# All tensor-tensor arithmetic of GpSimd to VectorE, and the squares of x behind its split, in a decoder layer on one core

## The chip, the core and the metric

The kernel runs on one core of a Trainium2 chip. The core has five engines with a queue of instructions each: TensorE (PE in the profile; its weight loads are PEld), VectorE (DVE), ScalarE (ACT), GpSimd (POOL) and SyncE (SP), which here issues most DMAs. Each engine works through its queue in order; engines wait for each other by semaphores. The metric is the device time of one execution in microseconds (us), lower is better. Runs are compared by the median.

## The reference, cut to what matters

A decoder layer on 256 tokens of width 2048, in float32. Three stages follow each other, each with a normalization before and after it and a residual addition.

```python
h = rms_norm(x, mix_pre_norm)
proj = h @ w_in                                   # 2048 x 10536
mlstm_p, rwkv_p, gate_p = split_cols(proj, ...)
ha = sigmoid(o) * norm(mlstm_chunkwise(q, k, v, ig, logf))          # 4 heads, chunks of 64
hb = (groupnorm(rwkv7_scan(r, decay, kr, v, kk, kk * a)) + bonus) * g   # 16 heads of 64
y = (sigmoid(g_a) * (ha @ w_branch_a) + sigmoid(g_b) * (hb @ w_branch_b)) @ w_out
x = x + rms_norm(y, mix_post_norm)

h, m = rms_norm(x, xattn_pre_norm), rms_norm(mem, mem_norm)
x = x + rms_norm(softmax(q(h) @ k(m).T) @ v(m) @ wo, xattn_post_norm)   # 4 heads of 128, 256 memory tokens

h = rms_norm(x, ffn_pre_norm)
u = causal_conv3(h @ w_up)                        # 2048 x 16384
x = x + rms_norm((gelu(gate(u)) * up(u)) @ w_down, ffn_post_norm)      # 8192 x 2048
```

`rms_norm` needs the sum of squares of each token over 2048 features. In the kernel a token's scale is applied behind the product, so that the products with w_in can begin before the sum is known.

## The kernel before, in words

**Precision.** Each large product is made of three products in the fast float32 format: a weight tile `raw` from DMA is rounded to `wh` by ScalarE (line 344), VectorE makes the remainder `wl = raw - wh` (line 353), and TensorE adds up wh*xh, wh*xl and wl*xh, where xh and xl are the same split of the activation (`hh`, `hl` for x in the first stage; `qh`, `ql` behind the first residual, `fh`, `fl` behind the second).

**Weight tiles and blocks.** `run` walks a list of blocks. A block is a piece of a weight matrix; its weights come as tiles of 128 x 1024 (128 x 768 in the first block), which I number through the program. Tiles 0 to 7 are the small columns of w_in (block "sm", 18 products a tile); 8 to 103 the projections r, k, v, q and k of the mLSTM, its v and its o (two blocks of 8 tiles each); 104 to 199 the gates and the two branch products, of which branch b begins with tile 168; 200 to 231 w_out; 232 to 239 the key of the cross-attention, 240 to 247 its query, 248 to 255 its value, 256 to 263 its output; 264 to 519 the FFN's up projection (32 blocks of 8 tiles); 520 to 647 its down projection. Most tiles cost 24 products with 256 columns. `run` stages wh and wl three tiles ahead of the products; there are 3 buffers for raw and 4 each for wh and wl. A block's PSUM banks come from four called acc; a block needs two, so before a block is begun, `run` calls `side.need` for the evacuation of the block two before.

**The side work.** Everything else (evacuations, gates, the chunked mLSTM, the RWKV scan, softmax, statistics, residuals) is written as Python generators. `Spread` decides, while the program is being written, where their pieces stand between the products. At each half of a tile `half` adds 600 to a budget for VectorE and 820 for ScalarE. A piece of the first waiting bulk generator, or else of one of the first two of `back`, is written while both budgets are above 0; pieces of `chains` are written every so many halves as long as the budgets are above -700. What a piece costs is counted by `Meter`, which wraps ScalarE and VectorE (`act`, `dve`) and adds a fixed part and a part per element to `spent`. GpSimd (`pool`) is not wrapped. `need` writes all that is left of a generator at once, at the place where it is called:

```python
    def need(self, s):
        while s and not s["done"]:
            if s in self.bulk:
                self._piece(self.bulk[0])
            ...
```

`need_hb` calls it for both halves of `rwkv` and for `hb_split` in front of the block of tile 168; `need_o` for the softmax and its product with the values in front of tile 256; `run` for the evacuation of the first up block in front of tile 280.

**Where GpSimd computes.** In `x_piece` (line 455) it squares the eight pieces of x and adds up the squares in st0. In `k_group` (line 704), run four times, it makes four products: KR, k2 and two halves of BK. In `gates` it multiplies a mask into pw, in `mlstm` it adds two parts of pw. In `Residual` (line 1181) it adds z to the stream xr for six of eight parts, and in `Stat.add` (line 257), called from there with `pool`, it adds up the squares of the new stream (stx, stf). At the end of the kernel it makes one of the eight last additions (line 1590). Apart from these it makes the power -0.5 of `rstd_of` (line 225), small copies and memsets, and issues the loads of `gup` in `hb_split` (line 1085).

`pre_sm` (line 470) orders the first block: for each piece of x a split into hh and hl on ScalarE and VectorE, then the squares on GpSimd, with the loads of x and of the weights on SP between. `sm_evac` (line 504) finishes the statistics (`finish`: one sum on VectorE, a product with ones on TensorE, `rstd_of`, a product that spreads the row) and reads the first block's banks.

`rwkv` (line 853) is written once for each half of the heads. Each pair of chunks ends in a group normalization: sum, subtraction, squares (ScalarE), sum, power (GpSimd), product, transposes (TensorE), scaling (ScalarE) and an addition to `bv`. When both halves are through, `hb_split` starts: split of gl, loads of gup, their split into gwh and gwl, four products zg, and for each a product with bv and the split into hb.

Of the kernel before, what the change touches and what calls it, by code (L numbers as in the profile page):

```python
# [11 lines left out]
AF = mybir.ActivationFunctionType  # L12
ALU = mybir.AluOpType
# [132 lines left out]
def _layer(ctx, tc, nc, d, dbg):  # L146
    act, dve = Meter(nc.scalar, 200.0, 0.83), Meter(nc.vector, 70.0, 1.04)
    pool, pe, sp = nc.gpsimd, nc.tensor, nc.sync
# [42 lines left out]
    xq = [x0[c // 4][:, c % 4 * 2:c % 4 * 2 + 2] for c in range(8)]  # L191
# [5 lines left out]
    def pcol(n, i=0, w=1):  # L197
        return par[:, PC[n] + i:PC[n] + i + w]

    def ccol(n, w, o=0):  # L200
        return con[:, CC[n] + o:CC[n] + o + w]

    ident = ccol("id", 128)
    E2 = [slice(0, 64), slice(64, 128)]
# [34 lines left out]
    def bc(ap, n):  # L239
        return ap.unsqueeze(1).broadcast_to((ap.shape[0], n, ap.shape[1]))  # L240

    class Stat:
# [11 lines left out]
        def square(self):  # L254
            return C("sq", f"{self.sq}{self.n % 2}", [P, 2, S])

        def add(self, src, eng=None):
            if self.n == 0:
                self.start()
                act.activation(self.acc, src, AF.Square)  # L260
            else:
                q = self.square()
                act.activation(q, src, AF.Square)
                (eng or dve).tensor_add(self.acc, self.acc, q)
            self.n += 1

        def fold(self):
# [185 lines left out]
    st0 = Stat("st0")  # L453

    def x_piece(c):
        for j in range(2):
            split_gain(hh[:, c * 2 + j], hl[:, c * 2 + j], xq[c][:, j], pcol("mixg", c * 2 + j))
        if c == 0:
            st0.start()
            pool.tensor_mul(st0.acc, xq[c], xq[c])  # L460
        else:
            q = st0.square()
            pool.tensor_mul(q, xq[c], xq[c])
            pool.tensor_add(st0.acc, st0.acc, q)
        st0.n += 1

    def x_load(c):
        sp.dma_start(xq[c], d["x"][:, c * 2:c * 2 + 2])
# [1 line left out]
    def pre_sm(ci, feed):  # L470
        if ci == 0:
            keep_warm(12)
            for c in range(3):
                x_piece(c)
                feed.lo(c)
                feed.dma(c + 3)
                x_load(c + 4)
            x_load(7)
        if ci + 3 < 8:
            x_piece(ci + 3)  # L480
        if ci == 4:
            sp.dma_start(con, d["con"])

# [6 lines left out]
    M, tasks = {}, {}  # L490
# [13 lines left out]
    def sm_evac(ps):  # L504
        dve.tensor_scalar(om, pcol("mu", 0, 27), -1.0, 1.0, op0=ALU.mult, op1=ALU.add)
        dve.tensor_scalar(oka, pcol("ka", 0, 8), -1.0, 1.0, op0=ALU.mult, op1=ALU.add)
        yield from st0.finish(3)
        pr = PR()
        dve.tensor_mul(pr, ps[0], bc(st0.rb, 2))
        wa, gl = C("wa", "m0"), T2("gl")  # L510
        gl0, gl1 = gl[:, 0], gl[:, 1]
        shiftmix(wa, pr[:, 0], 24)
        shiftmix(gl0, pr[:, 1], 25)
        yield
        pr = PR()
        dve.tensor_mul(pr[:, 0], ps[1][:, 0], st0.rb)
        shiftmix(gl1, pr[:, 0], 26, slice(0, 32))
        R = [T2("rows") for _ in range(4)]
        M["rows"] = R
        tasks["gates"] = side.add(gates(), chain=1)  # L520
        act.copy(R[0][0:4, 0], pr[32:36, 0])
        act.copy(R[0][0:4, 1], pr[64:68, 0])
        act.activation(wa[0:64], wa[0:64], AF.Tanh)
        tasks["smr"] = side.add(sm_rest(wa, gl0, gl1), back=True)
        yield
# [41 lines left out]
    def gates():  # L567
# [19 lines left out]
        src, alt = R4[4], R4[5]  # L587
# [72 lines left out]
        for o in (0, 256):  # L660
            for e in range(2):
                v = pw[E2[e], :, o + e * 64:o + e * 64 + 64]
                pool.tensor_mul(v, v, bc(ccol("im", 64)[E2[e]], 4))
            pool.memset(pw[E2[1], :, o:o + 64], 0.0)
        yield

# [37 lines left out]
    def k_group(p0):  # L704
        yield from side.patience(tasks["smr"], 60)
        KR, BK, at, lw, rr = M["KR"], M["BK"], M["at"], M["lw"], M["rr"]
        ss = slice(p0, p0 + 2)
        yield from side.patience(tasks["gates"], 60)
        if p0 == 0:
            tables("natural_log_exp_and_others")  # L710
        if p0 % 4:
            kt = U("kt", [P, 4, 2, S])
            k2, kk, nr, ep = (kt[:, i] for i in range(4))
        else:
            kt = [C("kt", f"au{i}", [P, 2, 2, S]) for i in range(2)]
            k2, kk, nr, ep = (kt[i // 2][:, i % 2] for i in range(4))
        kr = BK.rearrange("p a c s t -> p a (c s t)")[:, ss, 0:S]
        f8 = lambda v: v.rearrange("p a (c t) -> p (a c) t", c=4)
        KR8, BK8 = (v[:, ss].rearrange("p a c s t -> p (a c) s t") for v in (KR, BK))
        cum = lw[:, ss]  # L720
        for j in range(2):
            dve.tensor_tensor_scan(cum[:, j], seg, cum[:, j], 0.0, op0=ALU.mult, op1=ALU.add)
        for j in range(2):
            act.activation(kk[:, j], kr[:, j], AF.Identity, scale=pcol("kk", p0 + j))
        act.activation(nr, kk, AF.Square)
        q = yield from head_sums("ssk", nr)
        dve.tensor_scalar(nr, q, 1e-24, None, op0=ALU.max)
        act.activation(ep, cum, AF.Exp, scale=DECAY)
        yield
        act.activation(nr, nr, AF.Ln)  # L730
        act.activation(nr, nr, AF.Exp, scale=-0.5)
        yield
        for j in range(2):
            act.activation(k2[:, j], at[:, p0 + j], AF.Identity, scale=pcol("ka", p0 + j), bias=oka[:, p0 + j:p0 + j + 1])
        dve.tensor_mul(kk, kk, nr)
        pool.tensor_mul(KR8[:, :, 1], f8(rr[:, ss]), f8(ep))
        dve.scalar_tensor_tensor(KR8[:, :, 0, 1:64], f8(kk)[:, :, 1:64], -1.0, f8(ep)[:, :, 0:63],
                                 op0=ALU.mult, op1=ALU.mult)
        pool.tensor_scalar(KR8[:, :, 0, 0], f8(kk)[:, :, 0], -1.0, None, op0=ALU.mult)
        pool.tensor_copy(pce[:, ss], ep.rearrange("p a (c t) -> p a c t", c=4)[:, :, :, 63])  # L740
        pool.tensor_mul(k2, kr, k2)
        yield
        act.activation(nr, cum, AF.Exp, scale=-DECAY)
        dve.tensor_mul(kk, kk, at[:, ss])
        yield
        for e in range(2):
            dve.tensor_mul(BK8[E2[e], :, e], f8(kk)[E2[e]], f8(nr)[E2[e]])
            pool.tensor_mul(BK8[E2[e], :, 1 - e], f8(k2)[E2[e]], f8(nr)[E2[e]])
        yield
        for j in range(2):  # L750
            dve.scalar_tensor_tensor(rr[:, p0 + j], rr[:, p0 + j], pcol("rk", p0 + j), k2[:, j], op0=ALU.mult, op1=ALU.mult)
        yield
# [280 lines left out]
    def mlstm():  # L1033
        pw, vm, so = M["pw"], M["vm"], M["so"]
        M["pws"] = T2("pws")
        pool.tensor_add(M["pws"].rearrange("p a b -> p (a b)").rearrange("p (h q) -> p h q", h=4),
                        pw[:, :, 128:256], pw[:, :, 256:384])
        for t in range(2):
            js = [0] if t == 0 else [0, 1]
            qd = aux("den", [P, 4])  # L1040
# [137 lines left out]
    def part(v, k2):  # L1178
        return v[k2 // 4][:, (k2 % 4) * 2:(k2 % 4) * 2 + 2]

    class Residual:
# [8 lines left out]
        def run(self):  # L1190
# [24 lines left out]
            def scale(i):  # L1215
                dve.tensor_mul(part(z, i), part(z, i), bc(rb, 2))

            def add(i, eng):
                eng.tensor_add(part(xr, i), part(xr, i), part(z, i))  # L1219

            if self.early:
                yield
# [7 lines left out]
            yield  # L1230
            for i in range(1, 8):
                if i == 1:
                    add(1, dve)
                if i < 7:
                    scale(i + 1)
                    add(i + 1, pool)
                parts(i)
                if i == 1 and not self.early:
                    side.more()
                if self.early:  # L1240
                    self.st2.add(part(xr, i - 1), pool)
                elif i == 6:
                    self.stats = side.add(self.squares(0), chain=1)
                yield
# [3 lines left out]

        def squares(self, i0):
            for i in range(i0, 8):  # L1250
                self.st2.add(part(M["xr"], i), pool)
                yield
            for _ in range(2):
                yield
            yield from self.st2.finish(2)
# [307 lines left out]
    def fd_evac(n):  # L1563

        def gen(ps):
# [19 lines left out]
            def result(t, c):  # L1585
                f = slice(c % 2 * 512, c % 2 * 512 + 512)
                x, z_ = M["xt"][c // 2][:, t, f], M["z3", c // 2][:, t, f]
                if t and c == 1:
                    act.activation(z_, z_, AF.Copy, scale=rco[:, t:t + 1])
                    pool.tensor_add(x, x, z_)  # L1590
                else:
                    dve.scalar_tensor_tensor(x, z_, rco[:, t:t + 1], x, op0=ALU.mult, op1=ALU.add)
                (act if t and c != 1 else sp).dma_start(d["out"][t, :, c * 512:c * 512 + 512], x)

            if n == 0:
# [121 lines left out]
```

## Time and profile before

| | |
|---|---|
| median of 3 runs | 1953.44 us (1952.64 to 1955.28) |
| the profiled execution | 1954.48 us |
| its span from first to last instruction | 1952.6 us |
| mean granted clock of TensorE | 0.995 |
| busy: TensorE, VectorE, ScalarE, GpSimd | 1914.5, 1345.7, 1001.2, 136.7 us |
| instructions on VectorE, ScalarE, GpSimd | 1789, 1434, 127 |
| read from HBM | 347.73 MB, 179 GB/s over the span |

The profile is one execution. A row of the timeline has the start, the duration, the engine, the source line and the operation, then "out<-in" by the program's names, the shape and the count; in brackets stands how long the engine was idle before and what ended that. Nearly all rows of ScalarE and VectorE have line 66, that of Meter's wrapper, so that names and shapes tell them apart. A row of the groups has busy time and mean duration in ns of one. "A <- B: 16.1, 13, 2.2" among the waits means that A waited 16.1 us for B in 13 waits, the longest 2.2 us. Chain rows have start, length and count.

### The profile page before, as it was taken

To read this page: it belongs to the slowest core of one execution; us is meant where nothing else is said; L and a number is where in the kernel's file an instruction comes from. 1 tells how busy PE (TensorE), PEld (TensorE's weight loads), DVE (VectorE), ACT (ScalarE), POOL (GpSimd) and SP (SyncE) were. 2 spreads that over 40 slices of the span, in tenths; PEclk is the share of its full clock that TensorE was granted. 3 is DMA by queue.
4 is the path that set the end of the run, shared out by engine and by line. 5 is a ranking of instruction groups with operands and counts; after the bars stand their busy time and mean duration, and the time that the engine had idled before them with its cause. 6 is when DMAs were issued, how large, how long until landed. Compare 5 with 4: busy or idle time off the path is not lost.

```text
span 1952.6 us, 36537 instructions
## 1 busy us (share of the span) xinstructions
PE 1914.5 (98%) x15084; PEld 1805.1 (92%) x15084; DVE 1345.7 (69%) x1789; ACT 1001.2 (51%) x1434; POOL 136.7 (7%) x127
## 2 busy tenths in 40 slices
PE   8999999999999999899999999999999999999998
PEld 7999986999999999888999999999999998888886
DVE  6879888575566665867767666776667675556555
ACT  4776434454454564555555445544454454445443
POOL 4213100000010000304000000000000000000000
PEclk8999999999999999999999999999999999999999
DMA  6555645344455675435555655555655655655554
GB/s 205 170 163 168 182 156 162 109 152 141 132 190 180 214 256 182 159 132 172 173 184 189 197 196 192 189 194 195 194 195 185 199 190 200 207 188 191 187 191 151
DMA packets 97606, 352.20 MB, mean 180 GB/s; under 512 B 10880, under 2 KB 11136, under 8 KB 97056
## 3 DMA queue, kind: packets, MB, share of 16 engines
q1 hardware_dynamic: 96496, 348.07, 54.5%
q8 instruction: 118, 1.93, 0.4%
q10 hardware_dynamic: 720, 1.15, 0.2%
q0 software_dynamic: 224, 0.66, 0.1%
q14 instruction: 48, 0.39, 0.1%
HBM read 347.73 MB, written 2.10 MB: 179 GB/s over the span
## 4 chain that ended last, share of the span: by engine, by line
PE 88%; DVE 6%; issue 2%; DMA 2%; ACT 2%; POOL 1%; SPq 0%; DVEq 0%; ACTq 0%; POOLq 0%
PE fm L181 62%; PE tm L181 21%; DVE wl L353 2%; DVE tmp L66 1%; DMA raw<-in_w_in_dram 1%; ACT wh L344 1%; DVE fl L66 1%; PE Y L181 1%; DVE hl L66 1%; DMA raw<-in_w_fu_dram 0%; PE gram L181 0%; PE lv L181 0%; DVE z L66 0%; DMA raw<-in_w_sm_dram 0%; POOL xr L1219 0%
## 5 line engine op out<-in xcount | busy, mean ns | idle before, releaser
L353 DVE TENSOR_TENSOR wl<-raw,wh 128x1024 fp32r<-128x1024 f32 (+1 forms) x648 | 810.4, 1252 | 445.5 <-ACT wh L344 441.9
L344 ACT CAST wh<-raw 128x1024 fp32r<-128x1024 f32 (+1 forms) x648 | 675.1, 1044 | 573.9 <-PE fm L181 378.6
L181 PE MATMUL fm<-fl,wh 128*128 128x256 f32 x2048 | 568.0, 277 | 1.4 <-DVE fl L66 1.3
L181 PE MATMUL fm<-fh,wh 128*128 128x256 f32 x2048 | 568.5, 278 | 0.8 <-ACT fh L66 0.8
L181 PE MATMUL fm<-fh,wl 128*128 128x256 f32 x2048 | 567.5, 277 | 1.0 <-DVE wl L353 1.0
L181 PEld LDWEIGHTS fm<-fl,wh 128*128 128x128 f32 x2048 | 385.2, 188 | 2.2 <-DVE fl L66 2.2
L181 PEld LDWEIGHTS fm<-fh,wl 128*128 128x128 f32 x2048 | 385.3, 188 | 1.2 <-DVE wl L353 1.2
L181 PEld LDWEIGHTS fm<-fh,wh 128*128 128x128 f32 x2048 | 385.4, 188 | 1.0 <-ACT fh L66 1.0
L181 PE MATMUL tm<-wh,as 128*128 128x512 f32 x1024 | 318.6, 392 | 0.0
L181 PE MATMUL fm<-hh,wl 128*128 128x256 f32 x1072 | 302.3, 282 | 10.9 <-DVE wl L353 10.9
L181 PE MATMUL fm<-hh,wh 128*128 128x256 f32 x1072 | 306.7, 286 | 1.2 <-ACT wh L344 1.2
L181 PE MATMUL fm<-hl,wh 128*128 128x256 f32 x1072 | 301.4, 281 | 0.0
L181 PEld LDWEIGHTS tm<-wh,as 128*128 128x128 f32 x1024 | 192.2, 188 | 43.6
L181 PEld LDWEIGHTS fm<-hh,wl 128*128 128x128 f32 x1072 | 204.0, 190 | 12.9 <-DVE wl L353 12.9
L181 PEld LDWEIGHTS fm<-hh,wh 128*128 128x128 f32 x1072 | 204.1, 190 | 4.6 <-ACT wh L344 1.7
L181 PEld LDWEIGHTS fm<-hl,wh 128*128 128x128 f32 x1072 | 204.1, 190 | 0.0
L181 PE MATMUL tm<-wl,as 128*128 128x512 f32 x512 | 201.0, 393 | 0.0
L181 PEld LDWEIGHTS tm<-wl,as 128*128 128x128 f32 x512 | 96.1, 188 | 21.7
L66 ACT CAST as<-ac 128x256 fp32r<-128x256 f32 x128 | 45.6, 404 | 118.1 <-PE tm L181 118.0
L66 DVE TENSOR_TENSOR as<-ac,as 128x256 fp32r<-128x256 f32 x128 | 48.6, 422 | 66.6 <-ACT as L66 66.5
L225 POOL TENSOR_TENSOR rco<-var,mhalf 128x1 f32<-128x1 f32 x2 | 1.1, 550 | 1019.9 <-DVE var L66 1019.9
L181 PE MATMUL fm<-mgh,wh 128*128 128x256 f32 x256 | 71.4, 279 | 0.0
(363 smaller groups left out, 2341.7 us busy)
## 6 DMA issues: line engine op xcount, KB each, us to landing
raw<-in_w_fu_dram SPq DMA_DIRECT2D x256, 512.0 KB, 4.3
raw<-in_w_in_dram SPq DMA_DIRECT2D x160, 512.0 KB, 3.6
raw<-in_w_fd_dram SPq DMA_DIRECT2D x128, 512.0 KB, 4.3
raw<-in_w_br_dram SPq DMA_DIRECT2D x32, 512.0 KB, 3.8
raw<-in_w_mo_dram SPq DMA_DIRECT2D x32, 512.0 KB, 3.9
raw<-in_w_xk_dram SPq DMA_DIRECT2D x8, 512.0 KB, 4.3
raw<-in_w_xq_dram SPq DMA_DIRECT2D x8, 512.0 KB, 3.7
raw<-in_w_xv_dram SPq DMA_DIRECT2D x8, 512.0 KB, 3.6
```

Source lines behind the costliest of these rows:

```text
L66: return f(out, *a, **k)
L181: pe.matmul(out, lhsT, rhs, start=start, stop=stop, skip_group_check=True)
L225: pool.tensor_tensor(out, v, mhalf[:, 0:out.shape[1]], op=ALU.pow)
L344: nc.scalar.copy(wh, r)
L353: nc.vector.tensor_sub(wl, r, self.st[self.nl][0])
```

## The change

Three things are done. Each GpSimd operation with two tensors as inputs (but for the power in `rstd_of`) is issued on VectorE with the same operands. The squares of x go out of `x_piece`: `st0.add` makes them on ScalarE and adds them up on VectorE, for the pieces 0 to 5 in `pre_sm` at the tiles 5 to 7, when all pieces have been split, and for 6 and 7 at the beginning of `sm_evac`, a piece of side work each. And the last addition of line 1590 with the scaling before it becomes the one VectorE operation that the other seven results have.

```diff
         def add(self, src):
             ...
                 q = self.square()
                 act.activation(q, src, AF.Square)
-                (eng or dve).tensor_add(self.acc, self.acc, q)
+                dve.tensor_add(self.acc, self.acc, q)
     def x_piece(c):
         for j in range(2):
             split_gain(hh[:, c * 2 + j], hl[:, c * 2 + j], xq[c][:, j], pcol("mixg", c * 2 + j))
-        if c == 0:
-            st0.start()
-            pool.tensor_mul(st0.acc, xq[c], xq[c])
-        else:
-            q = st0.square()
-            pool.tensor_mul(q, xq[c], xq[c])
-            pool.tensor_add(st0.acc, st0.acc, q)
-        st0.n += 1
...
         if ci + 3 < 8:
             x_piece(ci + 3)
+        else:
+            for c in range((ci - 5) * 2, (ci - 5) * 2 + 2):
+                st0.add(xq[c])
...
     def sm_evac(ps):
...
+        for c in (6, 7):
+            st0.add(xq[c])
+            yield
         yield from st0.finish(3)
...
-                pool.tensor_mul(v, v, bc(ccol("im", 64)[E2[e]], 4))
+                dve.tensor_mul(v, v, bc(ccol("im", 64)[E2[e]], 4))
...
-        pool.tensor_mul(KR8[:, :, 1], f8(rr[:, ss]), f8(ep))
+        dve.tensor_mul(KR8[:, :, 1], f8(rr[:, ss]), f8(ep))
...
-        pool.tensor_mul(k2, kr, k2)
+        dve.tensor_mul(k2, kr, k2)
...
-            pool.tensor_mul(BK8[E2[e], :, 1 - e], f8(k2)[E2[e]], f8(nr)[E2[e]])
+            dve.tensor_mul(BK8[E2[e], :, 1 - e], f8(k2)[E2[e]], f8(nr)[E2[e]])
...
-        pool.tensor_add(M["pws"]..., pw[:, :, 128:256], pw[:, :, 256:384])
+        dve.tensor_add(M["pws"]..., pw[:, :, 128:256], pw[:, :, 256:384])
...
-            def add(i, eng):
-                eng.tensor_add(part(xr, i), part(xr, i), part(z, i))
+            def add(i):
+                dve.tensor_add(part(xr, i), part(xr, i), part(z, i))
...
-                    add(i + 1, pool)
+                    add(i + 1)
...
-                    self.st2.add(part(xr, i - 1), pool)
+                    self.st2.add(part(xr, i - 1))
...
-                self.st2.add(part(M["xr"], i), pool)
+                self.st2.add(part(M["xr"], i))
...
             def result(t, c):
-                if t and c == 1:
-                    act.activation(z_, z_, AF.Copy, scale=rco[:, t:t + 1])
-                    pool.tensor_add(x, x, z_)
-                else:
-                    dve.scalar_tensor_tensor(x, z_, rco[:, t:t + 1], x, op0=ALU.mult, op1=ALU.add)
+                dve.scalar_tensor_tensor(x, z_, rco[:, t:t + 1], x, op0=ALU.mult, op1=ALU.add)
```

More of the change, by code (lines that the diff above doesn't have):

```diff
@@ L255, in square, with add @@
             return C("sq", f"{self.sq}{self.n % 2}", [P, 2, S])
-        def add(self, src, eng=None):
+        def add(self, src):
             if self.n == 0:
@@ L1035, in mlstm @@
         M["pws"] = T2("pws")
-        pool.tensor_add(M["pws"].rearrange("p a b -> p (a b)").rearrange("p (h q) -> p h q", h=4),
-                        pw[:, :, 128:256], pw[:, :, 256:384])
+        dve.tensor_add(M["pws"].rearrange("p a b -> p (a b)").rearrange("p (h q) -> p h q", h=4),
+                       pw[:, :, 128:256], pw[:, :, 256:384])
         for t in range(2):
@@ L1232, in run @@
                 if i == 1:
-                    add(1, dve)
+                    add(1)
                 if i < 7:
                     scale(i + 1)
-                    add(i + 1, pool)
+                    add(i + 1)
                 parts(i)
```

## The prediction

> **What bounds the kernel now.** I read the page's shares first, then the waits of TensorE, then its busy time in windows, then the timelines of the places where it is idle.
>
> ```profile
> PE 1914.5 (98%) x15084; PEld 1805.1 (92%) x15084; DVE 1345.7 (69%) x1789; ACT 1001.2 (51%) x1434; POOL 136.7 (7%) x127
> PE 88%; DVE 6%; issue 2%; DMA 2%; ACT 2%; POOL 1%; SPq 0%; DVEq 0%; ACTq 0%; POOLq 0%
> PE fm L181 <- DVE wl L353: 16.1, 13, 2.2
> PE st L181 <- DVE stf L66: 2.4, 1, 2.4
> 585.16 130.32 PE fm L181 x1128
> ```
>
> TensorE is busy for 98% of the span and carries 88% of the chain that ended last. The change touches none of its products, so the time can move only where TensorE stands still: 1952.6 - 1914.5 = 38 us in all. It mostly waits for VectorE's weight remainder (wl). The last row prices its work: 130.32 / 1128 = 0.1155 us a product, 2.8 us for a weight tile of 24. Where it stands:
>
> ```profile
> 0.00:36.60 36.60, 27.67 (x169) 0.86 0.59 191
> 165.00:170.00 5.00, 2.99 (x26) 1.00 0.34 108
> 170.00:175.00 5.00, 5.00 (x31) 0.66 0.70 215
> 300.00:330.00 30.00, 26.12 (x120) 1.00 0.48 154
> 800.00:816.20 16.20, 11.03 (x88) 1.00 0.40 136
> 875.00:900.00 25.00, 21.76 (x175) 1.00 0.32 106
> ```
>
> The columns are the stretch, its length, TensorE's busy time, its matmuls, the granted clock, the DMA share and GB/s. The stops sit at the start, near 167, around 300 to 330 (the inverses), and in the two residual stages. All but the third lie where GpSimd works beside VectorE.
>
> **The change part by part.** First what VectorE pays for GpSimd's company, in the first block:
>
> ```profile
> 17.86 2.68 DVE L66 SCALAR_TENSOR_TENSOR hl<-x,par,hh 128x256 fp32r<-128x256 f32 x2
> 20.34 1.32 POOL L464 TENSOR_TENSOR st<-st,sq 128x512 f32<-128x512 f32 x1
> 20.47 2.01 DVE L353 TENSOR_TENSOR wl<-raw,wh 128x768 fp32r<-128x768 f32 x1
> 30.20 0.95 DVE L353 TENSOR_TENSOR wl<-raw,wh 128x768 fp32r<-128x768 f32 x1
> 31.07 0.87 DVE L66 SCALAR_TENSOR_TENSOR hl<-x,par,hh 128x256 fp32r<-128x256 f32 x2
> 31.86 0.95 DVE L353 TENSOR_TENSOR wl<-raw,wh 128x768 fp32r<-128x768 f32 x1
> ```
>
> With GpSimd active a piece of x costs VectorE 2.68 + 2.01 = 4.7 us; with GpSimd quiet (after 28 us) it costs 31.86 - 30.20 = 1.66 us. TensorE needs 18 x 0.1155 = 2.1 us for a piece, so today VectorE sets the pace and the 144 products of the block end only at 36.6 us (169 matmuls there, 24 of them warm-up). After the change VectorE needs 1.66 a piece and TensorE sets the pace: first product at 7.2, about 0.9 us for the first remainder, then 144 x 0.1155 = 16.6, so about 24.7, a gain of 11.9. Two things eat into it: the loads must come faster, and eight squares on ScalarE with seven additions on VectorE (0.6 us each) now stand between the weight tiles 8 to 12. They fit into ScalarE's idle time there, and cost at most some 1 us. I take -10.5, with -12 and -4 as ends (loads at 191 GB/s bring 5.3 MB only by 30 us).
>
> The operations in k_group: four products of 512 columns and two mask lines. Without GpSimd beside it VectorE needs 0.6 us for each. The stop at 165 to 170 (2.0 us) and the slower clock behind it, (1 - 0.66) x 5 = 1.7 us, should go: -3.7. At 300 to 330 GpSimd is idle, and VectorE has the same 31 growing steps after the change; they only come some 16 weight tiles later: 0, between -3.9 and +4.
>
> The early residual, between the key and the query block:
>
> ```profile
> 776.15 0.68 DVE L66 TENSOR_TENSOR z<-z,stb 128x512 f32<-128x512 f32 x1
> 776.75 0.88 DVE L66 SCALAR_TENSOR_TENSOR ql<-xr,par,qh 128x256 fp32r<-128x256 f32 x2
> 777.81 1.22 DVE L353 TENSOR_TENSOR wl<-raw,wh 128x1024 fp32r<-128x1024 f32 x1 [0.19 <-ACT wh L344]
> 778.96 0.68 DVE L66 TENSOR_TENSOR xr<-xr,z 128x512 f32<-128x512 f32 x1
> 789.62 1.91 DVE L66 SCALAR_TENSOR_TENSOR ql<-xr,par,qh 128x256 fp32r<-128x256 f32 x2
> 789.78 1.47 POOL L1219 TENSOR_TENSOR xr<-xr,z 128x512 f32<-128x512 f32 x1 [1.76 <-DVE z L66]
> 791.46 2.32 DVE L353 TENSOR_TENSOR wl<-raw,wh 128x1024 fp32r<-128x1024 f32 x1
> ```
>
> A part now takes 0.6 + 1.9 + 2.3, about 4.7 us with starts overlapping. Afterwards it is z, xr, ql, the statistics' addition and wl: 0.6 + 0.6 + 0.8 + 0.6 + 1.15 = 3.75 us. That is above TensorE's 2.8, but eight parts run up 8 x 0.95 = 7.6 us, less than the three weight tiles (8.3 us) by which run() stages ahead. The 16.2 - 11.0 = 5.2 us go. The late residual has no statistics: 0.6 + 0.6 + 0.8 + 1.15 = 3.15 a part against 3.56 now; of its 3.2 us about 2.0 go.
>
> **What the accounting does.** Meter adds to spent for ScalarE and VectorE alone. What moves from GpSimd becomes visible to Spread, which then gives side work out more slowly. The order of the changed program's instructions shows the result: whole chains that stood between products now stand in one lump, directly in front of the block that needs them. The first lump is the hand-over to branch b (weight tile 168). All of the end of rwkv for both halves and the whole of hb_split stand there; before, only the last two zg groups did. Its steps:
>
> ```profile
> 541.99 0.68 DVE L66 TENSOR_REDUCE gv<-bg 128x8 f32<-128x512 f32 x1
> 543.02 2.51 POOL L225 TENSOR_TENSOR gr<-var,mhalf 128x8 f32<-128x8 f32 x1 [3.32 <-DVE var L66]
> 546.24 0.69 DVE L66 TENSOR_TENSOR ysb<-ysb,gr 128x512 f32<-128x512 f32 x1
> 548.76 1.50 ACT L66 ACTIVATE bg<-yT,par 128x128 f32<-128x128 f32 x4 [0.87 <-PE yT L975]
> gup<-in_g_up_dram POOLq DMA_DIRECT2D x2, 256.0 KB, 5.5
> 566.26 1.78 ACT L66 CAST gwh<-gup 128x512 fp32r<-128x512 f32 x3
> 578.02 0.62 ACT L66 CAST hb<-vT 128x512 fp32r<-128x512 f32 x1 [1.89 <-DVE vT L66]
> 578.67 0.69 DVE L66 TENSOR_TENSOR hb<-vT,hb 128x512 fp32r<-128x512 f32 x1 [0.69 <-ACT hb L66]
> 583.24 1.91 PE zg L181 x16
> ```
>
> From TensorE's last product before it: about 0.9 for VectorE's previous remainder, then gv 0.7, power 0.3 + 2.5, product 0.7, transposes 0.6, four scalings 1.5, addition 0.7, and some 0.3 of hand-offs: 8.2. The other half follows in VectorE's order, 7.3 more, so 15.5. The loads of gup are issued behind the second power, at 11.7, and land 5.5 later, at 17.2; casts and remainder bring 19.4, two zg groups 21.3. The products with zg, cast and remainder of two groups end at about 23.9 for ScalarE, which then casts the second gup (1.8, 25.7); its remainder at 26.0, the last two zg groups at 28.0. Of this 1.2 of transposes and 3.8 of zg are TensorE's own work and stood elsewhere before: 23 us of stop. The clock: after a stop of 2 us this trace shows 5 us at 0.66. I add 3 us for zg and the first products at a lower clock: +26, between 20 and 31.
>
> The second lump is the softmax in front of weight tile 256. Statistics of the early residual end later, so four heads stand there in a row:
>
> ```profile
> 825.08 1.02 PE L181 MATMUL xsc<-kT,qT 128*128 128x256 f32 x4
> 827.12 1.28 ACT L66 ACT_TABLE_LOAD   x1 [1.01 <-DVE mx L66]
> 830.19 0.68 DVE L66 TENSOR_REDUCE mx<-xsc 128x2 f32<-128x512 f32 x1
> 832.96 0.69 DVE L66 TENSOR_REDUCE mx<-xsc 128x2 f32<-128x512 f32 x1
> L181 PE MATMUL xsc<-kT,qT 128*128 128x256 f32 x16 | 4.1, 379 | 0.0
> L181 PE MATMUL xo<-pT,xv 128*128 128x256 f32 x16 | 4.0, 392 | 0.1
> L1414 PE MATMUL xpT<-con,spr 128*128 128x128 f32 x16 | 2.4, 275 | 0.4 <-DVE spr L66 0.4
> ```
>
> The first scores come after 1.6 us, their maximum at 2.5; from the table load to the second head's maximum it is 830.19 - 827.12 = 3.1, so 5.6; then 832.96 - 830.19 = 2.8 a head, the fourth maximum at 11.2; its exponentials, scaling and transposes end at 14.7; xo ends at 18.7. TensorE's own share is 4.1 + 2.4 + 4.0 = 10.5, so 8.2 of stop, and 3 for the clock: +11.2, between 7 and 16.
>
> Two smaller ones. At weight tile 72 the banks of the first query block are read later than before, two remainders and two such products behind the last k_group's: +1.6. In front of tile 280 the statistics of the FFN input are forced, with four additions: about 4 us of stop where now the wait for stf (2.4) and that for its power stand: 0, between -1 and +2. At the very end one addition leaves GpSimd: -0.4.
>
> The sum: 26 + 11.2 + 1.6 - 10.5 - 3.7 - 5.2 - 2.0 - 0.4 = +17.0. The profiled execution took 1954.5 us (span 1952.6, the rest around it), so 1971.5; the runs' median, 1953.4, lies 1.0 lower: 1970.
>
> The clock is the term that I know least. The Trainium skill, page TensorE: Matmul & The Clock Gate, section "What's actually happening", says that the array falls to half its clock after about one idle window of 3.4 us and needs a busy one to come back. By that rule each lump would pay its own products at half rate and up to 3.4 us of products behind it, an estimate of 1.7 us for each such window. The trace agrees as far as it goes, with 0.66 over 5 us behind the stop at 167; no row of it has a stop of 10 us.
>
> **The rivals.**
> Faster: the first lump costs little. The place is tile 168, the condition that its two halves and the gup loads run beside each other and beside products, so that TensorE stops for less than 26 - 17 = 9 us. At no cost the time is 1944. For it speaks that VectorE and ScalarE have spare time (69% and 51% busy); against it that VectorE's order puts the second half behind the first, and that every engine there waits for the next.
> Colder: at half clock TensorE's 15.5 us in the two lumps take twice as long, and most of that lies on the path, since it alternates with the others: some +10, 1980. For it speaks the 0.66, against it that several stops of 1.5 us between 800 and 816 left the clock at 1.00.
> Loads: the first block is then bound by DMA and gains 4, not 10.5: 1976. The 191 GB/s there is a mean over a time in which the loads waited for buffers, which speaks against it.
> Half price: both lumps are pushed back only partly, and cost half, 18.6 less: 1951, no change.
>
> **How the numbers follow.** Forecast 0.58, colder 0.16, loads 0.08, half price 0.08, first lump free 0.10. The range 1955 to 1986 takes in the ends of the two lumps and of the start, and leaves out the free lump, part of half price and the top of colder, about 0.2. A difference below 0.2% (3.9 us) can't be told from none here. Slower takes the first three and a little of half price, 0.84; same 0.05, faster 0.11. The forecast's own range is 1961 to 1980.
>
> **What would show it.** Right: GpSimd's rows are powers and small copies; wl of 768 columns takes 0.95 from the start; the 144th product of the first block ends near 25 to 27 us; no stop of TensorE near 800; one stop of 20 to 30 us, in pieces, in front of the first product that reads hb, one of about 8 in front of the first that reads oT, with a clock well below 1 in both. Wrong: the first product with hb follows the last one with hh within 10 us, or VectorE's wl ends later than today somewhere in the long up and down projections, where no instruction changes place.

## The result, and the profile after

The changed kernel takes 1979.15 us (median, 1977.83 to 1980.73), the kernel before on the same chip 1953.04 us (1949.84 to 1955.28): a ratio of 1.0131, with a 95% interval of 1.0119 to 1.0143. It is 26 us slower; 17 were forecast. The profiled execution has a span of 1978.9 us. Its first rows, engine by engine, and the chain that ended last:

```profile
PE 1926.5 (97%) x15084; PEld 1814.6 (92%) x15084; DVE 1328.4 (67%) x1844; ACT 1006.2 (51%) x1441; POOL 42.8 (2%) x64
PE 80%; DVE 4%; ACT 2%; issue 1%; POOL 0%; DMA 0%; DVEq 0%; POOLq 0%; ACTq 0%
```

TensorE's idle time went from 38 to 52.4 us, and its busy time rose by 12.0 us for the same 15084 instructions, so products ran slower too. VectorE is busy for 17.3 us less, though it runs 55 instructions more: without GpSimd beside it, they are shorter on average. What TensorE waited for:

```profile
PE yT L974 <- DVE ysb L66: 9.9, 2, 5.7
PE xpT L1413 <- DVE spr L66: 6.5, 4, 3.2
PE zg L181 <- ACT gwh L66: 5.5, 2, 3.2
PE fm L181 <- DVE wl L353: 3.4, 7, 0.8
PE st L181 <- DVE stf L66: 3.1, 1, 3.1
PE gram L181 <- DVE bg L66: 2.8, 2, 2.4
PE tm L181 <- DVE kT L66: 2.5, 1, 2.5
PE tm L181 <- DVE qk L66: 2.4, 1, 2.4
PE den L181 <- DVE rd L66: 1.3, 1, 1.3
```

The wait for wl, 16.1 us before, is down to 3.4. In its place stand waits inside the side work: the transposes of rwkv's tail (yT), the softmax (xpT), the products of hb_split (zg).

To apportion the 26 us, I numbered the weight tiles in both traces and took for each stretch of tiles TensorE's loss: the gaps between its products, and by how much each product exceeds the median of its kind before. What moves from one stretch to another without loss drops out.

| tiles | before | after | change | forecast | uncharged (below) | charged (below) |
|---|---|---|---|---|---|---|
| 0 to 23, start | 17.1 | 7.0 | -10.1 | -10.5 | 6.4 | 15.3 |
| 48 to 55, k_group | 3.7 | -0.3 | -4.0 | -3.7 | -0.3 | -0.3 |
| 56 to 91, banks at 72 | 1.3 | 5.1 | +3.8 | +1.6 | 1.3 | 6.4 |
| 92 to 165, inverses, mlstm, rwkv | 21.2 | 27.0 | +5.8 | 0 | 21.4 | 23.6 |
| 166 to 179, first lump | -0.2 | 22.7 | +22.9 | +26 | -0.2 | 24.2 |
| 240 to 247, early residual | 6.1 | 2.3 | -3.8 | -5.2 | 1.2 | 6.2 |
| 248 to 257, second lump | 1.5 | 12.0 | +10.5 | +11.2 | 1.5 | 10.6 |
| 258 to 271, late residual | 5.6 | 5.0 | -0.5 | -2.0 | 4.5 | 6.0 |
| 272 to 287, FFN statistics | 4.9 | 6.9 | +2.0 | 0 | 0.3 | 10.8 |
| the rest | 4.0 | 4.0 | 0 | -0.4 | 4.0 | 4.0 |
| sum | 65.2 | 91.7 | +26.5 | +17.0 | 39.9 | 106.7 |

One row needs care. What is left after the change in tiles 240 to 247 (2.3) is no stop of the residual: it is the wait of 2.5 us for kT, in front of the first product of tile 248, whose PSUM bank the late evacuation of the key block (kT) still has to read.

The windows that answer to those of before:

```profile
0.00:26.10 26.10, 23.33 (x168) 22.29 (x169) 16.03 (x27) 18.04 (x32) 1.44 (x12) 1.00 0.78 260
150.00:200.00 50.00, 50.00 (x435) 50.00 (x435) 41.15 (x56) 33.33 (x49) 2.32 (x4) 1.00 0.59 183
300.00:330.00 30.00, 29.37 (x147) 24.31 (x146) 29.55 (x30) 12.93 (x14) 0.00 (x0) 1.00 0.50 150
375.00:380.00 5.00, 4.44 (x25) 4.25 (x26) 2.97 (x7) 0.67 (x1) 0.00 (x0) 0.50 0.57 195
580.00:585.00 5.00, 1.09 (x4) 0.71 (x4) 1.57 (x4) 2.02 (x5) 0.44 (x1) 0.50 0.00 0
595.00:600.00 5.00, 2.54 (x9) 1.69 (x8) 3.32 (x6) 2.89 (x5) 0.00 (x0) 0.50 0.00 0
600.00:605.00 5.00, 5.00 (x30) 5.00 (x31) 2.31 (x4) 1.60 (x3) 0.00 (x0) 0.65 0.01 3
800.00:820.00 20.00, 20.00 (x174) 20.00 (x174) 19.51 (x29) 14.43 (x23) 0.00 (x0) 1.00 0.49 163
865.00:870.00 5.00, 2.84 (x12) 2.28 (x10) 2.55 (x7) 2.18 (x6) 0.00 (x0) 0.63 0.01 3
```

The columns are the stretch, its length, then busy time and count of TensorE, its weight loads, VectorE, ScalarE and GpSimd, the granted clock, the DMA share and GB/s. The first block's 144 products end at 26.1 us in place of 36.6; the stops of k_group, at 300 to 330 and at 800 are gone. The new stops are near 580 and 860, at a granted clock of 0.50 near 580 and of 0.63 from 865 to 870, with a smaller one near 375. The first lump in the timeline (start, duration, engine, line, operation, operands; idle before):

```profile
575.77 0.28 PE L181 MATMUL fm<-hh,wl 128*128 128x256 f32 x1
577.75 1.64 POOL L225 TENSOR_TENSOR gr<-var,mhalf 128x8 f32<-128x8 f32 x1 [107.65 <-DVE var L66]
580.26 1.09 PE L974 MATMUL yT<-con,ysb 128*128 128x128 f32 x4 [4.21 <-DVE ysb L66]
584.56 1.64 POOL L225 TENSOR_TENSOR gr<-var,mhalf 128x8 f32<-128x8 f32 x1 [5.17 <-DVE var L66]
586.14 0.78 POOL L1089 DMA_DIRECT2D gup<-in_g_up_dram  x1
590.72 1.78 ACT L66 CAST gwh<-gup 128x512 fp32r<-128x512 f32 x3
597.59 1.77 ACT L66 CAST gwh<-gup 128x512 fp32r<-128x512 f32 x3
602.79 0.63 PE L181 MATMUL fm<-hb,wh 128*128 128x256 f32 x2
```

The last product with hh ends at 576.05, the first with hb starts at 602.79: 26.7 us. In between the two halves follow each other (powers at 577.75 and 584.56), the load of gup stands behind the second power, and ScalarE casts the second half of gup only after its work for the first two zg groups.

### The profile page after: what moved, and what is told of

The parts are those of the page before. It is cut to its first block, busy times and chain, and to the rows that moved or that the text cites. A ratio compares the mean times of both kernels' runs of the same rounds, so it can differ in the third digit from the quotient of the medians.

```text
span 1978.9 us, 36515 instructions
## 1 busy us (share of the span) xinstructions
PE 1926.5 (97%) x15084; PEld 1814.6 (92%) x15084; DVE 1328.4 (67%) x1844; ACT 1006.2 (51%) x1441; POOL 42.8 (2%) x64
## 4 chain that ended last, share of the span: by engine, by line
PE 80%; DVE 4%; ACT 2%; issue 1%; POOL 0%; DMA 0%; DVEq 0%; POOLq 0%; ACTq 0%
PE fm L181 54%; PE tm L181 22%; DVE wl L353 1%; DVE tmp L66 1%; ACT wh L344 1%; PE Y L181 1%; PE gram L181 0%; PE lv L181 0%; PE xo L181 0%; PE U L181 0%; PE X L181 0%; PE zg L181 0%; PE gramA L181 0%; ACT spr L66 0%; ACT z L66 0%
## 5 line engine op out<-in xcount | busy, mean ns | idle before, releaser
L353 DVE TENSOR_TENSOR wl<-raw,wh 128x1024 fp32r<-128x1024 f32 (+1 forms) x648 | 789.1, 1220 | 464.4 <-ACT wh L344 463.6
L66 ACT CAST as<-ac 128x256 fp32r<-128x256 f32 x128 | 45.6, 404 | 118.7 <-PE tm L181 118.7
L181 PE MATMUL fm<-mgl,wh 128*128 128x256 f32 x256 | 71.2, 278 | 0.0
```

The source lines that it names most:

```text
L66: return f(out, *a, **k)
L181: pe.matmul(out, lhsT, rhs, start=start, stop=stop, skip_group_check=True)
L353: nc.vector.tensor_sub(wl, r, self.st[self.nl][0])
```

## The experiments

**The moved work without its charge.** The operations stay on VectorE and ScalarE, but bypass Meter, so that Spread's budgets do not see them. TensorE's instructions then have the order of before.

```diff
-        dve.tensor_mul(k2, kr, k2)
+        nc.vector.tensor_mul(k2, kr, k2)
```

and likewise for every other moved operation (for the squares of x, nc.scalar and nc.vector, and no extra piece in sm_evac); only the last addition, at the end of the kernel, stays charged.

> The changed kernel, with every moved operation on VectorE and ScalarE as there, but not added to the spent time by which side work is given out: TensorE's instructions then stand in the order of before. Theory (the loss is the order, not VectorE's load): no stop over 5 us in front of weight tiles 168 and 256, the gains at the start (10), near 167 (4), in the early (4) and the late residual (1 to 2) stay: 1953 - 20 = 1933, between 1929 and 1939. Rival (VectorE's queue with the moved work is what is late): stops of 10 us and more stay in front of 168 or 256, and the time is 1955 or more.

Measured: 1930.04 us against 1952.75, a ratio of 0.9884 (0.9869 to 0.9898). Page and waits:

```profile
PE 1904.5 (99%) x15084; PEld 1797.1 (93%) x15084; DVE 1327.0 (69%) x1844; ACT 1004.4 (52%) x1441; POOL 41.7 (2%) x64
PE tm L181 <- DVE wl L354: 3.9, 5, 1.1
PE st L181 <- DVE st L66: 2.5, 1, 2.5
PE fm L181 <- DVE wl L354: 1.6, 4, 0.6
PE xpT L1413 <- DVE spr L66: 0.4, 1, 0.4
```

Same instructions on the same engines as in the changed kernel, 49 us less. No lump is left: the waits of yT, zg and for stf are gone, and that of xpT is 0.4 us. VectorE carries the moved work without a lump. This version is faster than both kernels.

**The charge without the move.** The kernel before, GpSimd's operations on GpSimd, each adding to `dve.spent` what VectorE's would; TensorE's order is that of the changed kernel, product for product.

```diff
+    class Charged:   # calls nc.gpsimd
...
+                dve.spent += dve.fixed + dve.per * n
...
-        pool.tensor_mul(k2, kr, k2)
+        cpool.tensor_mul(k2, kr, k2)
...
+        for _ in range(2):   # sm_evac, the two pieces for squares of x
+            act.spent += act.fixed + act.per * 512
+            dve.spent += dve.fixed + dve.per * 512
+            yield
```

> The kernel before, with GpSimd's operations left on GpSimd, but charged to VectorE's spent time as the changed kernel charges them: TensorE's instructions stand in the order of the changed kernel. Theory: both lumps are there, with stops of together some 30 us and the clock near half in them, and none of the gains: 1953 + 26 (the measured loss) + 20 (the gains that the changed kernel has beside it) = 1999, between 1985 and 2010. Rival (VectorE's load): with the load back on GpSimd the time is 1953 to 1960.

Measured: 1996.21 us, a ratio of 1.0223 (1.0208 to 1.0238).

```profile
PE yT L994 <- DVE ysb L66: 9.9, 2, 5.7
PE fm L196 <- DVE wl L368: 9.5, 10, 1.9
PE st L196 <- DVE stf L66: 6.2, 1, 6.2
PE xpT L1433 <- DVE spr L66: 5.9, 3, 3.2
PE zg L196 <- ACT gwh L66: 5.5, 2, 3.2
```

The waits for yT and zg are equal to the tenth to those of the changed kernel, though no operation has changed its engine. With the run before this makes a square: at the order of before, moving the work brings 22.7 us, at the new order 17 (1996.2 to 1979.2); the new order costs 43.5 with the work on GpSimd and 49.1 with it on VectorE. The loss is the order, and the order comes from the charge.

**The squares of x alone**, uncharged, the rest as before.

```diff
     def x_piece(c):
...
-            pool.tensor_mul(q, xq[c], xq[c])
-            pool.tensor_add(st0.acc, st0.acc, q)
...
+            for c in range((ci - 5) * 2, (ci - 5) * 2 + 2):
+                square0(c)   # nc.scalar squares, nc.vector adds
```

> Only the first part: the squares of x go behind the split, to ScalarE and VectorE, without a charge, so that nothing else changes place. Theory: weight remainders of 768 columns take 0.95 us from the start, weight tile 8 begins at 26 in place of 36.6, and all later tiles 10 us earlier: 1943, between 1940 and 1946. Rival (the first block is bound by its loads, or the gain is lost at the next stop): 1948 to 1953.

Measured: 1945.28 us, a ratio of 0.9961 (0.9946 to 0.9976). In the profile tile 8 starts at 25.1 and every tile from 104 on 10.6 to 10.9 us earlier than before; over the runs the gain is 7.5. The profiled execution is the fastest of the four (1943.63). The gain is within what the theory gave, and no later stop eats it. Where it varies is behind a new wait for the sum of the squares (st) at tile 9: tile 16 starts at 50.9 us in the uncharged version, at 52.8 here and at 54.9 in the run with writes below, with the same order of products. The wait is alike in the three (2.5, 2.4 and 2.5 us). What differs is the granted clock behind it: 1.00 and 1.00 from 30 to 35 and from 35 to 40 us in the first, 0.82 and 0.83 here, 0.72 and 0.60 with the writes.

**The budget raised.** The changed kernel with one line changed:

```diff
-    RATE_D, RATE_A, CAP = 600.0, 820.0, 1200.0
+    RATE_D, RATE_A, CAP = 800.0, 820.0, 1600.0
```

> The changed kernel with one line of numbers changed: RATE_D 800 in place of 600 and CAP 1600 in place of 1200, so that the moved work, charged as it is, is given out as early as before. The zg products then stand in weight tiles 159 to 164 and the scores in 252 to 253. Theory: the two lumps (22 and 10 us) and most of the 10 us of other stops vanish: 1979 - 40 = 1939, between 1932 and 1947. Rival (VectorE cannot carry the moved work in time, wherever it is written): more VectorE work next to the weight remainders makes TensorE wait for wl, and the time stays above 1960.

Measured: 1939.68 us, a ratio of 0.9938 (0.9922 to 0.9955). Two constants turn a loss of 26 us into a gain of 13, with all the work on VectorE and all of it charged. What they would do to the kernel before, without the move, no run shows. By the table's method the two lumps cost -0.5 and 3.5 us here; what is left against the uncharged version is mostly in tiles 92 to 165 (28.1 against 21.4).

**Which charge makes which lump.** The uncharged version with the charge put back for one group of operations: those of k_group with the masks and pws, or those of the residuals.

```diff
-        nc.vector.tensor_mul(k2, kr, k2)      # first: k_group, masks, pws
+        dve.tensor_mul(k2, kr, k2)
```
```diff
-            def add(i, eng=nc.vector):        # second: Residual, and Stat.add from there
+            def add(i, eng=dve):
```

> The uncharged version, in which only the moved operations of k_group, the masks of pw and pws are charged. TensorE's order then has the rwkv tails and all of zg in front of weight tile 168, while the scores stay in 251 and 252. Theory (each lump belongs to the charges of its own chain): 1930 + 23 (the lump in front of 168 as in the changed kernel) + 4 to 10 (the stops between weight tiles 56 and 166) = 1957 to 1963, with none of the 10 at tile 256. Rival (the first lump costs what it does only together with the late statistics behind it, or VectorE's other work hides it here): below 1950.

> The uncharged version, in which only the residual's moved additions and those of its squares are charged. The scores then stand in front of weight tile 256 and the FFN statistics in front of 280; the first 240 weight tiles keep their order. Theory: 1930 + 10.5 (tile 256) + 6.5 (tile 280) = 1947, between 1941 and 1952. Rival (the statistics are late because VectorE is full there, not because of the charge): the uncharged version would have been late too, and this one differs by less than 4 from 1930.

Measured: 1957.19 us (ratio 1.0021, 1.0012 to 1.0031) and 1948.52 us (0.9975, 0.9965 to 0.9984). The waits, the first two rows of the first kernel around tile 168, the other two of the second between 800 and 960 us:

```profile
PE yT L974 <- DVE ysb L66: 9.0, 2, 5.7
PE zg L181 <- ACT gwh L66: 5.5, 2, 3.2
```
```profile
PE xpT L1413 <- DVE spr L66: 7.9, 4, 3.2
PE st L181 <- DVE stf L66: 3.1, 1, 3.1
```

By the table's method the first loses 22.2 in tiles 166 to 179 and 1.5 in 248 to 257; the second -0.2 and 12.3, and 6.3 in 272 to 287. The lumps are separate, each from the charges of its own chain. Their prices add up: 27.2 + 18.5 us over the uncharged version are 45.6 of the 49.1 that all charges cost. The third charge, that of the squares of x, was not tested alone.

**A warm TensorE in the first lump.** The changed kernel with products of constants in the waits.

```diff
+            if "lump" in M:               # rwkv, in front of yT
+                keep_warm(12 if hf else 9)
...
+            if "lump" in M and p2 % 2 == 0:   # hb_split, in front of zg
+                keep_warm(4 if p2 else 7)
```

> The changed kernel, with products of constants that nobody reads put into the waits of the first lump: 9 and 12 in front of the two yT transposes, 7 and 4 in front of the first and third zg group. Theory (the half clock is a consequence of the stops, and costs some 6 us there): the granted clock stays near 1 from 575 to 605, the zg products take half as long, the first product with hb comes about 3 us earlier and what follows starts at full clock: 1979 - 5 = 1974, between 1971 and 1977. Rival (the chain through VectorE, ScalarE and GpSimd sets the end, and the clock is only a companion): within 1.5 of 1979.

Measured: 1977.01 us, a ratio to the kernel before of 1.0125 (1.0110 to 1.0140). Windows and a wait:

```profile
580.00:585.00 5.00, 1.96 (x14) 1.79 (x14) 2.05 (x4) 0.39 (x1) 3.46 (x5) 0.91 0.09 16
585.00:590.00 5.00, 3.89 (x19) 3.32 (x19) 2.82 (x5) 4.24 (x10) 0.50 (x1) 0.75 0.34 116
595.00:600.00 5.00, 4.28 (x34) 3.97 (x33) 3.05 (x5) 1.52 (x4) 0.00 (x0) 1.00 0.00 0
PE yT L976 <- DVE ysb L66: 5.2, 2, 3.0
```

The clock stays at 0.75 to 1.00, and from the last product with hh to the first with hb it is still 24.4 us, against 26.7. The median falls by 2.1, between the two expectations; the intervals of the two ratios overlap, so the time alone does not prove it. My 5 us were the 6.6 of slower products. As the first product with hb comes only 2.3 us earlier, most of them must have lain beside the chain of VectorE, ScalarE and GpSimd and not on it. The chain is the price of the lump, the clock about a tenth of it, as far as a clock that was not held at 1.00 throughout can tell.

**What GpSimd's company costs.** The kernel with only the squares of x moved, and GpSimd made to do something of no use beside VectorE in the first block, into a tile that nobody reads: two products of two inputs a piece, five constant writes, or three copies.

```diff
+        for _ in range(2):                    # range(5), range(3)
+            pool.tensor_mul(idle_, xq[c], xq[c])
+            # or pool.memset(idle_, 1.0), or pool.tensor_copy(idle_, xq[c])
```

> Only the squares of x moved, but GpSimd multiplies each piece of x by itself twice, as often as before, into a tile that nobody reads. Theory (VectorE pays for GpSimd's company alone, whatever becomes of the result): hl takes 2.68 for two again and wl of 768 columns near 2.0, weight tile 8 starts near 36, and the gain of the first part is gone: 1953, between 1949 and 1956. Rival (the first block was late because of the chain of squares and additions or of the buffers): 1945, as without the extra work, within 2.

> Only the squares of x moved, and GpSimd beside VectorE in the first block as in the run before, but with five constant writes of 128x512 a piece, which read nothing from SBUF. Theory (VectorE's operations of two SBUF inputs lose to GpSimd's reads, not to its being busy): hl stays at 0.87 for two, wl of 768 columns at 0.95, weight tile 8 starts near 25, and the time is 1945, within 3. Rival (any work of GpSimd holds VectorE up): hl above 2, weight tile 8 above 32, 1950 or more.

> The same with three copies of the piece of x by GpSimd in place of the writes: one SBUF input each. Theory (one read is enough): hl between 1.5 and 2.7 for two while a copy runs, weight tile 8 between 28 and 36, the time 1948 to 1955. Rival (only GpSimd's operations of two inputs cost VectorE anything): hl 0.87, and 1945 as without the extra work.

Measured: products 1953.73 us (ratio 1.0003, 0.9993 to 1.0012), writes 1946.04 (0.9958, 0.9941 to 0.9974), copies 1949.65 (0.9980, 0.9971 to 0.9990). Tile 8 starts at 33.7, 25.7 and 29.1 us. For each kernel in this order two rows of VectorE and GpSimd's row:

```profile
12.83 2.44 DVE L66 SCALAR_TENSOR_TENSOR hl<-x,par,hh 128x256 fp32r<-128x256 f32 x2
15.19 1.79 DVE L353 TENSOR_TENSOR wl<-raw,wh 128x768 fp32r<-128x768 f32 x1
4.62 15.62 POOL L462 TENSOR_TENSOR idle<-x 128x512 f32<-128x512 f32 x12 [1.97 <-DMA x<-in_x_dram]
```
```profile
10.98 0.88 DVE L66 SCALAR_TENSOR_TENSOR hl<-x,par,hh 128x256 fp32r<-128x256 f32 x2
11.78 0.95 DVE L353 TENSOR_TENSOR wl<-raw,wh 128x768 fp32r<-128x768 f32 x1
2.70 23.27 POOL L462 MEMSET idle<- 128x512 f32 x40
```
```profile
13.02 1.58 DVE L66 SCALAR_TENSOR_TENSOR hl<-x,par,hh 128x256 fp32r<-128x256 f32 x2
14.52 1.36 DVE L353 TENSOR_TENSOR wl<-raw,wh 128x768 fp32r<-128x768 f32 x1
4.42 21.78 POOL L462 COPY idle<-x 128x512 f32<-128x512 f32 x24 [1.78 <-DMA x<-in_x_dram]
```

Of the gain of 7.5 us the useless products leave nothing, copies 2.9, and writes, as many microseconds of them as of products, 6.5, which is not distinguishable from 7.5. It is GpSimd's reading that costs VectorE, whether or not anyone waits for the result. The Trainium skill, page SBUF — State Buffer, section "Who interferes with whom", says that a VectorE instruction with two inputs from SBUF contends with a GpSimd instruction that reads SBUF and not with one that only writes it; the three runs agree, with 2.44 and 1.58 against 0.88.

## Why the prediction was right, and where it was not

The direction and the mechanism held: the gains of GpSimd's silence are real, and the order that the charge brings costs more. One premise did not hold, that the time can move only where TensorE stands still: of the 26.3 us by which the span grew, 14.3 are idle time and 12.0 are slower products. Term by term:

- **Start**, -10.5 forecast, -10.1 measured, wl at 0.95 to 0.96 from the start: right. Its reason, company alone, is shown by the useless products.
- **k_group**, -3.7 against -4.0: the size was right, the reason incomplete. With GpSimd's work in place and only the order changed the stop is gone too (-0.3 in the charged kernel), so here either of the two is enough.
- **First lump**, 26 against 22.9. The resume at 28.0 was 26.7. The power took 1.64 where I had taken 2.51 from a row of before, and all TensorE work there ran at half clock: gaps were 16.1 us where I had 23, slower products 6.6 where I had 3. The two errors partly cancel, so that the total is closer than its parts, partly by luck; products at half clock fill time in which TensorE would have waited, and the warm run got only 2.3 us of it back.
- **Second lump**, 11.2 against 10.5, the resume 18.7 against 20.1. Right, but the same late order also brought the wait of 2.5 us for kT in front of the value block, which the forecast did not have; it stands in the kernel with only the residuals charged too (2.4).
- **Early residual**, -5.2 against -3.8: all stops inside it are gone, so the term was if anything too small; what the row has left is that wait for kT. **Late residual**, -2.0 against -0.5: the gaps went from 4.0 to 1.4, but products slower than their kind from 1.6 to 3.7.
- **Banks at tile 72**, 1.6 against 3.8: a wait of 2.4 for qk and slower products behind it. Mis-sized.
- **Inverses: 0, "between -3.9 and +4"**. This is the step that failed most. The stop at 300 to 330 did go, with the slower products of tiles 92 to 103 a gain of 7.5, and it was the order that removed it: it is gone in the charged kernel and stands as before in the uncharged one. But I had looked only at the stop I could see, not at what the later order does to all that is planned behind the inverses: the mlstm and rwkv pieces of tiles 104 to 165 lost 13.3 us, in waits of gram, den and haT and a clock of 0.50 near 375. Together +5.8. The charged kernel has 2.4 of it, with GpSimd at work. Its gaps in tiles 104 to 165 are the same (6.1 us against 6.2, the wait for gram 2.5 against 2.4), so these too come from the order. The rest of the 5.8 is the clock: behind the wait for gram it is 0.50 and then 0.84 from 375 to 385 in the changed kernel, and stays at 1.00 in the charged one.
- **FFN statistics**, 0 against +2.0. I had set the new wait against the old one. The uncharged kernel shows that without the charge both would be gone (0.3 in 272 to 287), so the order costs 6.6 there and the move saves 4.6; the two terms hid in one zero.

Of the rivals, "colder" is nearest in time (1980), and wrong in its reason: the clock did fall to a half, but cost little. "Loads" is refuted by the start (-10.1): 260 GB/s came in there, where that rival had counted with 191, and even at 191 loads that end at 30 us would have left a gain of 36.6 - 30 = 6.6, not 4. "Half price" and "faster" are refuted by the lumps. The sum missed by 9.5 us in the table: +5.8, +2.2 and +2.0 for stops of the new order that I had set at zero or too low, +1.4 and +1.5 in the rows of the residuals, the first of them by the wait for kT, and -3.1 for the first lump.

## What to carry to other kernels

Where a program places its own instructions by an account of costs, moving work between engines changes two things, and they have to be priced apart: what the engines do, and what the account now sees. Test them as a square, with the move uncharged and the charge unmoved, before blaming an engine; here the move was worth 23 us at the order of before, and two constants of the budget decided whether it showed. And work on GpSimd is not free because GpSimd is idle: the 94 us of it that went away here had cost VectorE more time than it needs to do nearly all of that work itself.

## What the hardware showed that I had not expected

VectorE and GpSimd did not merely slow each other down, they took turns, one instruction for one. The first window lies beside the products, of which the program has two for every three instructions of VectorE, the second beside the copies, three for three. The counts (third and fifth in brackets) are 11 of VectorE and 10 of GpSimd, and 22 and 21:

```profile
8.76:20.98 12.22, 7.17 (x54) 6.56 (x54) 12.22 (x11) 6.33 (x12) 10.88 (x10) 1.00 0.56 187
7.46:26.93 19.47, 16.66 (x126) 15.26 (x126) 19.47 (x22) 12.96 (x23) 17.50 (x21) 1.00 0.70 230
```

The starts alternate: products at 10.99, 12.17 and 13.89 us, VectorE's instructions at 11.12, 12.83 and 14.01. Beside the writes nothing is paired, with 25 of them against 19 of VectorE from 8.44 to 22.40 us. So what an instruction of VectorE pays hardly depends on its own length: beside the copies hl costs 0.35 more each ((1.58 - 0.88) / 2) and wl, with three times the columns, 0.41; beside the products 0.78 and 0.84. Short operations suffer most in proportion. The Trainium skill, page SBUF — State Buffer, section "Who interferes with whom", has the rule that issue order decides who blocks; the alternating starts agree with it.

A stop in pieces kept the granted clock down as long as it lasted: waits of 4.2, 5.7, 3.2 and 2.2 us with 1.1, 1.1 and 4.6 us of products between them gave a granted clock of 0.50 for 20 us. The Trainium skill, page TensorE: Matmul & The Clock Gate, section "What's actually happening", gives half the clock after an idle window of about 3.4 us; the trace agrees as far as the first of these waits is longer than that. Shorter waits did it too, but not each time: 2.4 us for gram near 375 were followed by 0.50 over 5 us, 2.5 us for gram in the charged kernel by 1.00, and 2.4 to 2.5 us for st near 31 us by 1.00, 0.82 or 0.72 in three versions. Where these rows differ from the page, the rows decide. The price was small in the first lump, about 2 us of 23, where other engines held the path, and about 3 us behind gram, where products follow each other without a wait.
